# A decoder layer with two attentions: NSA's z gates computed in the phase of Strassen's products, and a third bank for NSA's logits

## The chip, the cores and the metric

The kernel runs on one core of a Trainium2 chip. PE multiplies matrices (its weight loads, PEld, run beside it), DVE and ACT work on elements, POOL and SP mostly issue DMAs here. The metric is the device time of one execution in microseconds (us); the time before is 1524.45, the median of three runs.

## The reference, cut to what matters

One layer on 512 tokens of width 2048, all in float32:

```
h   = x @ W_in                       # columns: fox q,k,v,f,z | nsa q, k,v (three branches), gates, z | merge a, b
y_a = (fox_attention(...) * silu(fox_z)) @ w_a
y_b = (nsa_attention(...) * silu(nsa_z)) @ w_b
x   = layer_norm(alpha * x + (sigmoid(merge_a) * y_a + sigmoid(merge_b) * y_b) @ w_o)
```

There are 8 heads of width 128 in each attention. NSA has two groups of four heads; a group shares its keys and values, and each head adds three branches: 31 compressed blocks, selected blocks and a window. With 512 tokens the selection and the window both see all earlier tokens. The change touches `nsa_z` (1024 columns of `W_in`, from column C_NZ), the last 256 columns of each merge gate, and the order of NSA's other projections.

## The kernel before, in words

**Numbers.** A float32 operand is kept as a high and a low part (`split`: ACT copies to the reduced format, DVE subtracts). A product is three matmuls (`mm3`): high by high, high by low, low by high. One matmul has a 128x128 stationary operand and up to 512 moving columns.

**Units.** The program is a list of units that `stream` emits in turn. A unit has a weight tile of 128x512, loaded by SP into `wr` and split into `wh`/`wl` three units ahead. `dense` (by way of `proj`) computes 128 columns of a projection for all 512 tokens, transposed (columns on partitions), as 16 k-tiles: four units of four k-tiles, 48 matmuls into one of two `d` banks, and then an evacuation function.

**Ticks.** All other work hangs on `tick()`, which `dense` calls after k-tiles 1 and 3 of each unit. A tick advances every job in `active` by one step, then the first entry of the queue `tq`, then that of `sq`. Steps are written as generators. So the order on each engine is fixed when the program is built: dense matmuls, then a tick's pieces, then dense matmuls. `drain(cond)` calls `tick` with no dense work between until a condition holds.

**A head of NSA.** `nsa_s` (in `sq`) waits for the head's q and its group's keys, and then emits eight matrix products of logits into `s` banks, one in a tick; a tick later `exp_row` (DVE adds the bias and takes the extreme, ACT the exponential), a tick later `norm_row`. `nsa_t` (in `tq`) has nine items, one in a tick: PE transposes a block of probabilities into a `pt` bank (two of them), a tick later `split_p` reads it with ACT and DVE into `pT`, two ticks later `pv` multiplies it with the values into bank `o`. At the end `gate_out` (L433) multiplies `o` with the head's gate tile `z`. In a tick a head's `pv` comes first, then `split_p`, then the next transpose.

**PSUM.** There are eight banks: `d`, `s` and `pt` two each, `o` and `m` one each. A bank is used again when the instructions that read it are done. `m` carries the transposes of V in `evac_v`.

**Gates.** silu is written as 0.5 z (1 + tanh(z/2)). Each NSA z projection comes right behind its head's q projection, and `evac_z` (L289) makes the gate from `d` with one ACT and one DVE instruction; it waits in one of five `z` tiles.

**The phase of products.** `pairs` computes 512 tokens by two column blocks of 512 (or 384), k in two halves, with Strassen's seven products in place of eight: 7 x 48 matmuls with the tokens' parts as stationary operands. DVE adds blocks of weights, POOL adds others by accumulating DMAs. Results come out by rows (tokens on partitions), pass through `zo` and are stored to DRAM by SP (`keep`). Before, it has five jobs: Fox's V into `vd`, and for each merge gate columns 0 to 1023 and 1024 to 1791 into `sig_d` after a sigmoid. The last 256 columns of each merge gate are four dense projections at NSA's end (`evac_sig`: sigmoid, four transposes into an `s` bank, ACT copy, store). Before the last of these, `o_open` (L1191) drains all jobs.

**Order.** First z of three Fox heads and raw compressed keys and values, then the phase of products, Fox, NSA, the merge (`y_chunk`), the output projection and the norm. NSA's order is q0, z0, keys and values of group 0 (`nsa_open` drains Fox first), then q and z of heads 1 to 3, keys and values of group 1, q and z of heads 4 to 7, four gate tiles. The new keys wait until the group's logits are done, the new values until its values stage is done.

Of the kernel before, what the change touches and what calls it, by code (L numbers as in the profile page):

```python
# [12 lines left out]
F32 = mybir.dt.float32  # L13
F32R = mybir.dt.float32r
AF = mybir.ActivationFunctionType
ALU = mybir.AluOpType
# [47 lines left out]
def layer(ctx, tc, x, w_in, b_f, pos_k, pos_v, wk1, wk2, wv1, wv2, w_a, w_b, w_o, ln_g, ln_b, rel, onehot, out):  # L64
# [147 lines left out]
                u["pre"] = pre  # L212
            units.append(u)

    def dense(w, ncols, col, rows, get_src, evac, pre=None, each=None):

        kts = rows // P
        st = {}

        def pe(u, k0):  # L220
            if k0 == 0:
                st["ps"] = bank("d", 2)
            hi, lo = (t.rearrange("p (k c) -> p k c", c=P) for t in u["w"])
            for k in range(4):
                if each:
                    each(k0 + k)
                mm3(st["ps"], (hi[:, k], lo[:, k]), get_src(k0 + k), k0 + k == 0, k0 + k == kts - 1)
                if k % 2 == 1:
                    tick()
            if k0 + 4 == kts:  # L230
                evac(st["ps"])

        for k0 in range(0, kts, 8):
            add_chunk(lambda r: r.rearrange("p (k c) -> p k c", c=P),
                      dram(w, k0 * P * ncols + col, [[ncols, P], [P * ncols, 8], [1, P]]),
                      lambda u, half, k0=k0: pe(u, k0 + 4 * half), pre=pre if k0 == 0 else None)
# [77 lines left out]
    def v_load(h):  # L314
# [11 lines left out]
        split(hi, lo, v)  # L326
        done.add(("v", ("f", h)))

    def evac_q(key):
        def f(p):  # L330
            take("q")
            t = pool("attn").tile([P, 2, S], F32R, name="q", tag="q", bufs=2)
            split(t[:, 0], t[:, 1], p, SC)
            qt[key] = t
            done.add(("q", key))
        return f
# [8 lines left out]
    def evac_v(key, dst):  # L345

        def f(p):
            take("vT")
            v = pool("attn").tile([P, S], F32, name="vT", tag="vT", bufs=1)
            nc.scalar.activation(v, p, AF.Copy)  # L350

            def job():
                yield
                yield
                m = bank("m", 1)
                for j in range(NT):
                    nc.tensor.transpose(m[:, j * P:(j + 1) * P], v[:, j * P:(j + 1) * P], ident)
                free["vT"] += 1
                hi, lo = dst()
                split(hi, lo, m)  # L360
                done.add(("v", key))
                yield
            active.append(job())
        return f
# [109 lines left out]
    def fox_bias(h):  # L474
# [7 lines left out]
                                    fill=NEG, base=i * P, channel_multiplier=1)  # L482
        return m

    def nsa_s(h, st):
        key, g = ("n", h), h // HPG
        yield from wait_for(("q", key), ("k", ("s", g)), ("k", ("w", g)))
        bt = pool("nsa").tile([P, S], F32, name="bt", tag="bt", bufs=2)
        nc.gpsimd.dma_start(bt, dram(skew_d, h * P * RL + P - 1, [[RL - 1, P], [1, S]]))  # L489
        yield  # L490
        st["s"], st["st"] = yield from take_p()
        st["w"], st["wt"] = yield from take_p()
        q, k = qt[key], kt_[g]
        tcm = pool("nsa").tile([P, NT, CP], F32, name="tc", tag="tc", bufs=1)

        def mm(it):
            i, br = it["i"], it["br"]
            n = (i + 1) * P
            t0 = slice(i * P, (i + 1) * P)
            b = bank("s", 2)  # L500
            it["bias"] = bt[:, (NT - 1 - i) * P:]
            if i == 0:
                def both(u):
                    return k[:, u, :2 * S].rearrange("p (b c) -> p b c", b=2)[:, :, :CP + P]
                mm3(b[:, :2 * (CP + P)].rearrange("p (b c) -> p b c", b=2), (q[:, 0, t0], q[:, 1, t0]),
                    (both(0), both(1)), True, True)
                it["b"], it["logits"] = b, b[:, CP:CP + P]
                it["other"].update(logits=b[:, 2 * CP + P:2 * (CP + P)], bias=it["bias"])
                return
            c0 = {"c": 0, "sc": 0, "s": CP, "w": CP + S}[br]  # L510
            nn = {"c": CP, "sc": CP + n, "s": n, "w": n}[br]
            mm3(b[:, :nn], (q[:, 0, t0], q[:, 1, t0]), (k[:, 0, c0:c0 + nn], k[:, 1, c0:c0 + nn]), True, True)
            it["b"] = b
            it["logits"] = b[:, CP:CP + n] if br == "sc" else b[:, :n]

        def red(it):
            if it["br"] in ("c", "sc"):
                nc.vector.tensor_tensor(tcm[:, it["i"]], it["b"][:, :CP], cb[:, h, it["i"]], op=ALU.add)
            if it["br"] != "c":
                exp_row(it)  # L520
            if "other" in it:
                exp_row(it["other"])

        def norm(it):
            if it["br"] != "c":
                norm_row(it)
            if "other" in it:
                norm_row(it["other"])

        def items(nm, n, brs):  # L530
            mn, l, r = stat("mn"), stat("l"), stat("r")
            return [dict(i=i, br=br, p=st[nm], mn=mn, l=l, r=r, gate=gates[:, i, 3 * h + n:3 * h + n + 1])
                    for i, br in brs]

        steps = items("s", 1, [(0, "sc"), (1, "sc"), (2, "sc"), (3, "c"), (3, "s")])
        other = items("w", 2, [(i, "w") for i in range(NT)])
        steps[0]["other"] = other[0]
        steps += other[1:]
        mc, lc, rc = stat("mn"), stat("l"), stat("r")
        for n, _ in enumerate(staged(steps, (mm, red, norm))):  # L540
            if n == 5:
                nc.vector.tensor_reduce(mc, tcm, axis=AX.X, op=ALU.max)
                nc.vector.tensor_tensor(tcm, tcm, mc[:, :, None].to_broadcast([P, NT, CP]), op=ALU.subtract)
                nc.scalar.activation(tcm, tcm, AF.Exp)
            if n == 7:
                nc.vector.tensor_reduce(lc, tcm, axis=AX.X, op=ALU.add)
                nc.vector.reciprocal(rc, lc)
                nc.vector.tensor_tensor(rc, rc, gates[:, :, 3 * h], op=ALU.mult)
                yield from take_later("tc")

                st["c"] = tc3 = pool("nsa").tile([P, NT, C3], F32, name="tc3", tag="tc3", bufs=1)
                nc.vector.tensor_tensor(tc3.rearrange("p i (u c) -> p i u c", u=3),
                                        tcm[:, :, None, :].to_broadcast([P, NT, 3, CP]),
                                        rc[:, :, None, None].to_broadcast([P, NT, 3, CP]), op=ALU.mult)
            if n == 7:
                done.add(("s", key))
                free["q"] += 1
            yield
        done.add(("p", key))
# [54 lines left out]
    zd = [dp.tile([P, S], F32, name=f"z_d{h}") for h in range(NZD)]  # L614
    rawd = {(kv, g): dp.tile([P, S], F32, name=f"raw_d{kv}{g}") for kv in "kv" for g in range(G)}
    vd = dp.tile([S, H * DH], F32, name="v_d")
    sigd = [dp.tile([S, D], F32, name=f"sig_d{g}") for g in range(2)]

    def tables():
# [291 lines left out]
            return t[:, 0].rearrange("p j d -> p (j d)"), t[:, 1].rearrange("p j d -> p (j d)")  # L911
        return f

    def nsa_kv(g):
        def vpre():
            drain(lambda: all(("t", ("n", h)) in done for h in range(g * HPG)))
        proj(C_KS + g * DH, evac_k(("s", g), nsa_k_dst("s", g)), pre=None if g else nsa_open)
        proj(C_KW + g * DH, evac_k(("w", g), nsa_k_dst("w", g)))
        proj(C_VS + g * DH, evac_v(("s", g), nsa_v_dst("s", g)), pre=vpre if g else None)
        proj(C_VW + g * DH, evac_v(("w", g), nsa_v_dst("w", g)))  # L920

# [196 lines left out]
    def phase_split():  # L1118
        jobs = [kept(vd, AF.Copy, C_FV, (0, S), S)]
        for g, c in enumerate((C_GA, C_GB)):  # L1120
            jobs.append(kept(sigd[g], AF.Sigmoid, c, (0, S), S))
            jobs.append(kept(sigd[g], AF.Sigmoid, c, (2 * S, 2 * S + W2), W2))
        ops = {n: t_op(n) for n in ("T1", "T2", "T3", "T4")}
        ops.update({"B11": b_op(0, 0), "B21": b_op(1, 0), "B22": b_op(1, 1)})
        pairs(jobs, ops, KT // 2, pairs_open)
# [30 lines left out]
    for kv, h in (("v", 4), ("k", 1)):  # L1156
        for n, l0 in enumerate(range(0, CMP_LEN, 2 * LB)):
            units[at[h] + 4 * n + 4:at[h] + 4 * n + 4] = cmp_units(kv, l0)
    for h in range(H):
        if h % HPG == 0 and h:  # L1160
            nsa_kv(h // HPG)
        proj(C_NQ + h * DH, evac_q(("n", h)))
        proj(C_NZ + h * DH, evac_z(("n", h)))
        if h == 0:
            nsa_kv(0)


    sig, osp, fin = {}, {}, {}

# [32 lines left out]
                    yield  # L1202
        active.append(job())

    for j in range(NG // P, KT):
        for g, c in enumerate((C_GA, C_GB)):
            proj(c + j * P, evac_sig(g, j), pre=o_open if (j, g) == (KT - 1, 1) else None)

    BANKS = [("pt", 2), ("pt", 2), ("o", 1), ("m", 1)], [("d", 2), ("d", 2), ("s", 2), ("s", 2)]

# [351 lines left out]
```

## Time and profile before

| | |
|---|---|
| median of 3 runs | 1524.45 us (1524.35 to 1525.06) |
| the profiled execution | 1525.12 us, its span 1523.4 us |
| PE busy | 1504.0 us, 99% of the span |
| DVE, ACT, POOL busy | 55%, 42%, 14% |
| granted PE clock | 0.999 |
| phase of products | 106 to 460 us |
| NSA, from the first q to the last gate tile | 767 to 1156 us |

The span is the time between the first and the last instruction; what lies around it is in the execution's time. A line of the timeline gives start, duration, engine, line of the kernel, operation, output and inputs, shape and count; in brackets stands the idle time of the engine ahead of it and who ended it. Successive matmuls overlap, so a matmul's price is the distance between two starts and not its duration. Instructions of one kind in a row are merged (x3).

### The profile page before, as it was taken

The page shows a single profiled execution, that of the slowest core. Times are in us where ns is not written, and L with a number is a line of the kernel's source. Part 1 is how long each engine was busy: PE and PEld are TensorE (multiplying, and loading weights), DVE is VectorE, ACT ScalarE, POOL GpSimd, SP SyncE. Part 2 cuts the span into 40 slices and gives each one's busy share as a digit, 9 for nine tenths or more (in the row PEclk, how much of TensorE's full clock was granted, in tenths as well). Part 3 has the DMA queues.
Part 4 walks back from the last instruction along what each step waited for, and adds up shares of the span by engine and source line. Part 5 has one row for each costly group of instructions (what it writes and reads, how often), then busy time and mean ns, then how long its engine had stood idle before and what let it go on. Part 6 is the DMA issues. An engine that isn't in the chain of part 4 may idle for free.

```text
span 1523.4 us, 19742 instructions
## 1 busy us (share of the span) xinstructions
PE 1504.0 (99%) x7161; PEld 1256.0 (82%) x7161; DVE 836.7 (55%) x1680; ACT 647.0 (42%) x1270; POOL 210.6 (14%) x351
## 2 busy tenths in 40 slices
PE   8999999999999999999999999999999999999998
PEld 6688788987998888888888888888888888888886
DVE  4566666666664654654435665366645444444455
ACT  6255656555563543533334444244444222222233
POOL 1211010111114623422000000000002010030001
PEclk9999999999999999999999999999999999999999
DMA  8678585877666443443233222322236343272236
GB/s 227 156 220 183 183 194 161 197 214 180 161 161 190 144 136 91 144 138 108 72 98 90 75 77 73 87 76 77 56 96 209 125 145 125 91 249 97 97 111 166
DMA packets 202929, 208.59 MB, mean 137 GB/s; under 512 B 12768, under 2 KB 153104, under 8 KB 202832
## 3 DMA queue, kind: packets, MB, share of 16 engines
q1 hardware_dynamic: 181936, 158.88, 34.9%
q0 software_dynamic: 20608, 47.93, 14.2%
q8 instruction: 56, 0.92, 0.2%
q10 hardware_dynamic: 288, 0.52, 0.1%
q14 instruction: 41, 0.34, 0.1%
HBM read 190.72 MB, written 20.22 MB: 138 GB/s over the span
## 4 chain that ended last, share of the span: by engine, by line
PE 92%; DVE 4%; ACT 2%; DMA 1%; issue 1%; POOL 0%; SPq 0%; ACTq 0%; DVEq 0%; POOLq 0%
PE d L105 50%; PE s L105 13%; PE pt L105 9%; PE o L105 9%; PE m L105 6%; DVE wl L97 2%; PE pt L417 2%; ACT wh L96 1%; PE m L111 1%; PE o L111 0%; PE d L1234 0%; DMA sig_d<-zo 0%; DVE c L993 0%; DVE s L992 0%; DMA vT<-v_d 0%
## 5 line engine op out<-in xcount | busy, mean ns | idle before, releaser
L105 PE MATMUL d<-big,wh 128*128 128x512 f32 x1792 | 568.7, 398 | 1.4 <-ACT wh L96 1.1
L97 DVE TENSOR_TENSOR wl<-wr,wh 128x512 fp32r<-128x512 f32 (+1 forms) x492 | 331.5, 682 | 379.1 <-ACT wh L96 368.7
L96 ACT ACTIVATE wh<-wr 128x512 fp32r<-128x512 f32 (+1 forms) x492 | 299.8, 618 | 388.5 <-PE d L105 140.0
L105 PEld LDWEIGHTS d<-big,wh 128*128 128x128 f32 x1792 | 324.1, 188 | 65.2 <-issue 2.1
L105 PE MATMUL d<-big,wl 128*128 128x512 f32 x896 | 351.5, 392 | 0.1
L105 PEld LDWEIGHTS d<-big,wl 128*128 128x128 f32 x896 | 168.5, 188 | 37.9 <-DVE wl L97 0.9
L399 ACT ACTIVATE p<-p,mn 128x128 f32<-128x128 f32 (+3 forms) x96 | 54.0, 562 | 133.5 <-DVE mn L397 133.5
L97 DVE TENSOR_TENSOR wl<-s,wh 128x512 fp32r<-128x512 f32 (+1 forms) x120 | 75.2, 637 | 54.1 <-ACT wh L96 53.9
L96 ACT ACTIVATE wh<-s 128x512 fp32r<-128x512 f32 (+1 forms) x120 | 69.0, 587 | 58.3 <-DVE wl L97 32.8
L105 PE MATMUL s<-wh,T 128*128 128x512 f32 (+1 forms) x320 | 93.2, 367 | 0.0
L105 PE MATMUL o<-wh,big 128*128 128x512 f32 (+1 forms) x224 | 84.3, 376 | 2.6 <-ACT wh L96 2.6
L105 PE MATMUL m<-wh,big 128*128 128x512 f32 (+1 forms) x224 | 83.7, 374 | 0.0
L105 PE MATMUL d<-wh,big 128*128 128x512 f32 (+1 forms) x240 | 74.4, 376 | 0.0
L97 DVE TENSOR_TENSOR pT<-pt,pT 128x512 fp32r<-128x512 f32 (+1 forms) x96 | 46.6, 488 | 44.3 <-ACT pT L96 43.9
L105 PEld LDWEIGHTS s<-wh,T 128*128 128x128 f32 x320 | 59.2, 188 | 7.5
L805 POOL TENSOR_SCALAR af<-raw,posT 128x31 f32<-128x31 f32 x128 | 65.2, 531 | 0.1
L96 ACT ACTIVATE pT<-pt 128x512 fp32r<-128x512 f32 (+1 forms) x96 | 41.2, 433 | 46.8 <-PE pt L417 46.0
L105 PE MATMUL s<-wl,T 128*128 128x512 f32 (+1 forms) x160 | 58.7, 367 | 0.0
L105 PEld LDWEIGHTS o<-wh,big 128*128 128x128 f32 x224 | 42.0, 188 | 10.6 <-ACT wh L96 4.5
L105 PEld LDWEIGHTS d<-wh,big 128*128 128x128 f32 x240 | 44.7, 188 | 7.2 <-ACT wh L96 0.4
L967 POOL DMA_DIRECT2D r<-in_w_in_dram x20 | 24.0, 1198 | 187.5 <-DVE wl L97 77.4
L489 POOL DMA_DIRECT2D bt<-skew_d x8 | 4.3, 540 | 324.9 <-DVE mn L397 257.5
(314 smaller groups left out, 2398.9 us busy)
## 6 DMA issues: line engine op xcount, KB each, us to landing
wr<-in_w_in_dram SPq DMA_DIRECT2D x147, 512.0 KB, 3.7
wr<-in_w_o_dram SPq DMA_DIRECT2D x32, 512.0 KB, 3.6
wr<-in_w_in_dram SPq DMA_DIRECT2D x24, 384.0 KB, 3.8
wr<-in_w_a_dram SPq DMA_DIRECT2D x16, 512.0 KB, 3.6
om<-sig_d POOLq DMA_DIRECT2D x32, 256.0 KB, 4.9
wr<-in_w_b_dram SPq DMA_DIRECT2D x16, 512.0 KB, 3.6
r<-in_w_in_dram SPq DMA_DIRECT2D x12, 512.0 KB, 5.3
r<-in_w_in_dram POOLq DMA_DIRECT2D x12, 512.0 KB, 10.4
```

The costliest lines, as they stand in the source:

```text
L96: nc.scalar.activation(hi, src, AF.Copy)
L97: nc.vector.tensor_tensor(lo, src, hi.bitcast(F32), op=ALU.subtract)
L105: nc.tensor.matmul(o, u, v, start=first and n == 0, stop=last and n == 2, **kw)
L111: nc.tensor.matmul(*u, start=first and u is whole, stop=last and u is whole)
L399: nc.scalar.activation(row, row, AF.Exp, bias=it["mn"][:, i:i + 1], scale=-1.0, accum_out=it["l"][:, i:i + 1])
L417: nc.tensor.transpose(b[:, (i - j) * P:(i - j + 1) * P], pt[:, OFF[i] + j * P:OFF[i] + (j + 1) * P], ident)
L489: nc.gpsimd.dma_start(bt, dram(skew_d, h * P * RL + P - 1, [[RL - 1, P], [1, S]]))
L805: nc.gpsimd.tensor_scalar(af[:, l, g], src, posT[:, po0 + ll:po0 + ll + 1], None, op0=ALU.add)
L967: nc.gpsimd.dma_start(two(n, k), rows(jobs[j], quad[0] * kh + k - 1, quad[1]), accum_op=ALU.add)
```

## The change

The eight z projections leave NSA. A sixth job of `pairs` computes nsa_z by rows and stores it, without an activation, to a new DRAM tensor `nz_d`. For each head a new job `nz_load` takes a `z` tile, loads the head's 128 columns (rows on partitions, 512 bytes each), waits four ticks, transposes four 128x128 blocks into a `pt` bank, and makes the gate as before (tanh on ACT, product on DVE). It is put into `active` ahead of the head's q projection.

NSA's projections have a new order: q0, one gate tile, keys and values of group 0, q1 to q4 with group 1's keys behind q4, q5, group 1's values, q6, q7, three gate tiles. The gate tiles and the last two q projections tick after k-tiles 1, 2 and 3. The logits take three banks in turn (`m`, `s`, `s`), and `evac_v` transposes into `pt` instead of `m`.

```diff
-    def dense(w, ncols, col, rows, get_src, evac, pre=None, each=None):
+    def dense(w, ncols, col, rows, get_src, evac, pre=None, each=None, steps=(1, 3)):
...
-                if k % 2 == 1:
+                if k in steps:
                     tick()
...
+    def rows_of(dt, ncols, col):
+        return dram(dt[:], col, [[ncols, P], [P * ncols, NT], [1, DH]])
+
+    def nz_load(h):
+        yield from take_later("z")
+        t = z_tile()
+        nc.gpsimd.dma_start(t.rearrange("p (j d) -> p j d", d=DH), rows_of(nzd, H * DH, h * DH))
+        for _ in range(4):
+            yield
+        m = bank("pt", 2)
+        for j in range(NT):
+            nc.tensor.transpose(m[:, j * P:(j + 1) * P], t[:, j * P:(j + 1) * P], ident)
+        nc.scalar.activation(t, m, AF.Tanh, scale=0.5)
+        nc.vector.scalar_tensor_tensor(t, t, 1.0, m, op0=ALU.add, op1=ALU.mult)
+        zt["n", h] = t
+        done.add(("z", ("n", h)))
+        yield
...
     def evac_v(key, dst):
...
-                m = bank("m", 1)
+                m = bank("pt", 2)
...
+    logits = [0]
+
+    def s_bank():
+        logits[0] += 1
+        return bank(*(("m", 1), ("s", 2), ("s", 2))[logits[0] % 3])
...
     def nsa_s(h, st):
...
-            b = bank("s", 2)
+            b = s_bank()
...
+    nzd = dp.tile([S, H * DH], F32, name="nz_d")
...
-    def nsa_kv(g):
+    def nsa_keys(g):
+        proj(C_KS + g * DH, evac_k(("s", g), nsa_k_dst("s", g)), pre=None if g else nsa_open)
+        proj(C_KW + g * DH, evac_k(("w", g), nsa_k_dst("w", g)))
+
+    def nsa_values(g):
...
+        jobs.append(kept(nzd, AF.Copy, C_NZ, (0, S), S))
...
-    for h in range(H):
-        if h % HPG == 0 and h:
-            nsa_kv(h // HPG)
-        proj(C_NQ + h * DH, evac_q(("n", h)))
-        proj(C_NZ + h * DH, evac_z(("n", h)))
-        if h == 0:
-            nsa_kv(0)
...
-    for j in range(NG // P, KT):
-        for g, c in enumerate((C_GA, C_GB)):
-            proj(c + j * P, evac_sig(g, j), pre=o_open if (j, g) == (KT - 1, 1) else None)
+    rest = [(j, g) for j in range(NG // P, KT) for g in range(2)]
+
+    def gate_tile(pre=None):
+        j, g = rest.pop()
+        proj((C_GA, C_GB)[g] + j * P, evac_sig(g, j), pre=pre, steps=(1, 2, 3))
+
+    for h in range(H):
+        proj(C_NQ + h * DH, evac_q(("n", h)), pre=lambda h=h: active.append(nz_load(h)),
+             steps=(1, 3) if h < H - 2 else (1, 2, 3))
+        if h == 0:
+            gate_tile()
+        if h % HPG == 0:
+            nsa_keys(h // HPG)
+        if h in (0, HPG + 1):
+            nsa_values(h // HPG)
+    while rest:
+        gate_tile(pre=o_open if len(rest) == 1 else None)
```

More of the change, by code (lines that the diff above doesn't have):

```diff
@@ L912, in nsa_v_dst @@
         return f
-    def nsa_kv(g):
+    def nsa_keys(g):
+        proj(C_KS + g * DH, evac_k(("s", g), nsa_k_dst("s", g)), pre=None if g else nsa_open)
+        proj(C_KW + g * DH, evac_k(("w", g), nsa_k_dst("w", g)))
+    def nsa_values(g):
         def vpre():
             drain(lambda: all(("t", ("n", h)) in done for h in range(g * HPG)))
-        proj(C_KS + g * DH, evac_k(("s", g), nsa_k_dst("s", g)), pre=None if g else nsa_open)
-        proj(C_KW + g * DH, evac_k(("w", g), nsa_k_dst("w", g)))
         proj(C_VS + g * DH, evac_v(("s", g), nsa_v_dst("s", g)), pre=vpre if g else None)
```

## The prediction

> **What bounds the kernel now.** I read the page first, then the waits of PE, then stretches of the timeline. The page's lines are PE's busy time, PE and its granted clock in 40 slices, and the chain that ended last.
>
> ```profile
> PE 1504.0 (99%) x7161; PEld 1256.0 (82%) x7161; DVE 836.7 (55%) x1680; ACT 647.0 (42%) x1270; POOL 210.6 (14%) x351
> PE   8999999999999999999999999999999999999998
> PEclk9999999999999999999999999999999999999999
> PE 92%; DVE 4%; ACT 2%; DMA 1%; issue 1%; POOL 0%; SPq 0%; ACTq 0%; DVEq 0%; POOLq 0%
> ```
>
> PE is busy for all but 19 us, at full clock, and is 92% of the chain. So the time changes by the matmul time that goes or comes, plus every wait that PE takes in its own order. Who PE waited for:
>
> ```profile
> PE s L1465 <- DMA xa<-in_x_dram: 4.5, 1, 4.5
> PE m L718 <- DVE facc L712: 1.3, 1, 1.3
> PE pt L417 <- DVE pT L97: 0.8, 2, 0.4
> PE s L1182 <- ACT z L1175: 0.7, 1, 0.7
> ```
>
> These are totals: PE waited only 0.8 us for a transpose bank (`pt`) in all 16 heads. NSA's stage has no slack to give back, and any new wait there is paid in full.
>
> **The matmul work.** The phase of products runs PE without holes; a 512-wide job ran twice in a row (vd, then the first of sig_d). The jobs begin where the bank changes to `pt`:
>
> ```profile
> 106.33 0.39 PE L105 MATMUL pt<-wh,T 128*128 128x512 f32 x1
> 184.12 0.39 PE L105 MATMUL pt<-wh,T 128*128 128x512 f32 x1
> 261.90 0.33 PE L105 MATMUL pt<-wh,T 128*128 128x384 f32 x1
> ```
> ```profile
> 106.33:184.12 77.79, 77.02 (x338) 62.92 (x336) 51.44 (x73) 43.56 (x72) 8.48 (x8) 1.00 0.74 187
> 184.12:261.90 77.78, 77.02 (x337) 62.92 (x336) 51.16 (x73) 44.42 (x74) 9.54 (x8) 1.00 0.71 178
> 1037.00:1070.00 33.00, 33.00 (x172) 27.95 (x171) 21.23 (x63) 14.83 (x37) 0.54 (x1) 1.00 0.28 72
> ```
>
> The columns are length, then busy time of PE, PEld, DVE, ACT and POOL. The new sixth job has the same shape (1024 columns as two blocks of 512): seven products of 48 matmuls. It costs **+77.8**, and its sums (DVE), POOL's accumulating loads, SP's reads and its eight writes to nz_d lie inside, as in these two.
>
> Eight NSA z projections of 48 matmuls go. One projection with little beside it is the last gate tile, from 1145.14 to 1156.12:
>
> ```profile
> 1143.65 0.39 PE L105 MATMUL d<-big,wl 128*128 128x512 f32 x1
> 1144.07 0.60 ACT L1175 ACTIVATE z<-d 128x512 f32<-128x512 f32 x1 [2.31 <-PE d L105]
> 1144.72 0.66 PE L1182 MATMUL s<-ident,z 128*128 128x128 f32 x4 [0.69 <-ACT z L1175]
> 1145.14 0.71 PE L105 MATMUL d<-big,wh 128*128 128x512 f32 x2
> 1145.48 0.60 ACT L1183 ACTIVATE z<-s 128x512 f32<-128x512 f32 x1 [0.81 <-PE s L1182]
> 1156.12 0.39 PE L105 MATMUL pt<-wh,osp 128*128 128x512 f32 x1
> ```
>
> That is 10.98 us (0.23 a matmul, 1.37 for the six between two ticks), so **-87.8**. Each gate is now transposed, four transposes of 128x128. Their price, from the transposes of a gate tile between other work:
>
> ```profile
> 1121.82 0.60 PE L1182 MATMUL s<-ident,z 128*128 128x128 f32 x4
> 1122.18 0.60 PE L105 MATMUL o<-pT,nvs 128*128 128x256 f32 x3
> 1122.52 0.60 ACT L1183 ACTIVATE z<-s 128x512 f32<-128x512 f32 x1 [2.45 <-PE s L1182]
> ...
> 1122.86 0.71 PE L105 MATMUL d<-big,wh 128*128 128x512 f32 x2
> 1123.01 0.59 ACT L96 ACTIVATE pT<-pt 128x512 fp32r<-128x512 f32 x1
> ```
>
> 0.36 to the next start, and the pair of dense matmuls behind transposes is shown 0.09 longer (0.71 here, 0.62 in the row of 1060.23 further down): 0.45, times eight **+3.6**. Work alone: 77.8 - 87.8 + 3.6 = **-6.4 us**.
>
> The eight loads of a gate (POOL) are issued ahead of their use by four ticks and more, since POOL stands idle in NSA's stage (0.54 us busy in the 33 us above): nothing. Nor does it count as work that eight tanh and products move from a projection's end to behind the transposes; their place in the order does, and is the next point.
>
> **Where PE now waits for a bank.** Ticks are counted through the generators. A head's values stage (`nsa_t`) takes 13 ticks: nine transposes into `pt` on ticks 1 to 9, each split one tick later, products on ticks 4 to 12. A gate is transposed on the fifth tick of its head's q projection, and this job runs ahead of `nsa_t` in the tick. Both share two `pt` banks. With KS0's first tick as 1: gates 1 to 7 fall on 37, 45, 53, 61, 86, 112 and 124; values of heads 0, 1, 3, 4, 5 transpose on 35 to 43, 53 to 61, 79 to 87, 110 to 118 and 123 to 131. So five gates (1, 4, 5, 6, 7) fall one tick behind a transpose whose bank is not yet split. Order on PE: gate's four transposes into the one free bank, perhaps a product, then the head's next transpose. That one needs a bank that is freed at the earliest by the gate's own tanh (ACT) and product (DVE), which stand ahead of the head's split on both engines. Gate 3 comes with its head's first transpose, and the dense matmuls of a tick (1.37 us) cover it; gates 0 and 2 meet none.
>
> The price of one meeting: 0.70 from the first transpose to ACT's start (1121.82 to 1122.52), 0.63 from tanh to the product and 0.69 for it (rows below), 0.05 to PE's restart (1144.67 to 1144.72): 2.07, less PE's own 0.45 and the product between.
>
> ```profile
> 1069.04 0.60 ACT L294 ACTIVATE z<-d 128x512 f32<-128x512 f32 x1
> 1069.67 0.69 DVE L295 SCALAR_TENSOR_TENSOR z<-z,d 128x512 f32<-128x512 f32 x1 [1.24 <-ACT z L294]
> ```
>
> Gates 1, 6, 7 meet no product: 1.6 each. Gate 4 has three 512-wide matmuls between (0.69): 0.9. Gate 5 has three 128-wide ones (0.28, from 1059.14 to 1059.42 further down): 1.35. Together **+7.1**. Ends: 0, if the banks free up unlike this count; 12, if each next transpose waits for the head's split too (0.69 more) and ACT is 0.3 late. Behind a waiting transpose stand the logits and the next dense matmuls, all on PE. The old z evacuation read `d`, which has two banks and never held PE.
>
> **The drains.** By the same count, ticks without dense work grow from 1 to 4 where NSA opens, 1 to 2 before VS1, 0 to 1 at KS1, 4 to 6 before the last gate tile. At NSA's opening a gate tile now ends just before: PE waits for the sigmoid as in the rows above, 1143.65 to 1144.72 instead of 0.23: **+0.85** (0.7 by that row's wait; 2.1 with a table load in front). The sigmoid's table comes twice more into ACT; ahead of it ACT stood idle for 2.31, and a load takes 1.28:
>
> ```profile
> 1114.74 1.28 ACT L1175 ACT_TABLE_LOAD   x1
> ```
>
> so nothing. [...]
>
> Before the last gate tile the wait of 0.85 was there already; now head 7's last three transposes, splits and products fill the same drain. By ACT's and DVE's order PE waits about 1.1: **+0.3** (0 to 2). The other two drains issue work whose splits are a tick old: 0.
>
> **Shorter ticks.** The last two q projections and the gate tiles tick three times per four k instead of two. While logits and values of two heads overlap, one tick hangs on a loop through ACT and DVE. In the kernel before:
>
> ```profile
> 1059.14 0.45 PE L105 MATMUL o<-pT,nvs 128*128 128x128 f32 x3
> 1059.42 0.40 PE L417 MATMUL pt<-ident,p 128*128 128x128 f32 x2
> 1059.58 0.81 PE L105 MATMUL s<-nk,q 128*128 128x416 f32 x3
> 1060.23 0.62 PE L105 MATMUL d<-big,wh 128*128 128x512 f32 x2
> ...
> 1062.34 0.49 PE L105 MATMUL s<-nk,q 128*128 128x32 f32 x3
> ...
> 1062.78 0.55 DVE L397 CUSTOM_DVE_ANT_0 p<-s,bt 128x384 f32<-128x384 f32 x1
> ...
> 1064.66 0.63 PE L105 MATMUL s<-nk,q 128*128 128x512 f32 x2
> ...
> 1065.77 0.68 DVE L397 CUSTOM_DVE_ANT_0 p<-s,bt 128x512 f32<-128x512 f32 x1
> ```
>
> DVE takes the logits of 1059.58 at 1062.78, 3.2 late, while PE's ticks are 2.5 apart (1059.58, 1062.34, 1064.66). In a short tick PE has 0.9 of dense work instead of 1.4, so some 2.0. Over the 11 overlapping short ticks (heads 6 and 7) DVE falls behind by up to 1.2 a tick; three logits banks instead of two give PE 6 us of lead, two `pt` banks 4. I take **+1.0** (0 to 4): half a microsecond for each overlap. Otherwise the third logits bank is worth nothing, since PE waited for no logits bank before; values at `pt` meet nothing (their head waits for them).
>
> **Fox's start.** ACT's split of the first v waits for POOL's load, which stands behind loads that wait for the last store of the products' phase:
>
> ```profile
> 473.75 0.63 ACT L96 ACTIVATE v<-vT 128x512 fp32r<-128x512 f32 x1 [9.88 <-DMA vT<-v_d]
> 474.96 0.73 PE L105 MATMUL d<-big,wh 128*128 128x512 f32 x2 [0.65 <-ACT wh L96]
> ```
>
> That store is now 512 wide instead of 384: **+0.3** (0 to 1).
>
> **Sum.** -6.4 + 7.1 + 0.85 + 0.3 + 1.0 + 0.3 = +3.15. The profiled execution took 1525.12 (span 1523.4 and 1.7 around it), so 1528.3; the median of the runs shown lies 0.67 lower, so **1527.6**.
>
> **Rivals.** *Faster: the banks are free in time.* If the meetings cost 0 to 2 us, the sum is -5 to -2: about 1520.5. For it: PE waited 0.8 us for `pt` before, and DVE is busy only 64% of an NSA stretch (21.23 of 33). Against: the order in a tick is fixed, and the rows of 1122.52 and 1123.01 show the split of a head's `pT` standing behind a gate's copy on ACT. *Slower: the loop of ACT and DVE bounds the short ticks.* Place: from NQ7 to the second gate tile. Each of 11 overlapping ticks at 3.2 instead of 2.0, less 4 us of lead once: +9, with the rest 1536. It decides as soon as the lag passes two ticks, when a transpose finds its `pt` bank unsplit. For it the 3.2 above; against it, the lag there fell to 1.1 two rows later. *The clock falls.* A wait that drops the granted clock would make each 512-wide matmul slower than its 0.23; the page shows full clock through waits of 4.5 and 1.3. [...] *The job is no cheaper than the projections* is excluded by two jobs at 77.8.
>
> **Chances.** Forecast 0.53, own range 1524 to 1532; banks free 0.27; loop bound 0.17; clock 0.03. Runs of this kernel tell 0.2% (3 us) from no change: slower is above 1527.5, faster below 1521.4. The forecast lies on that line, half of it slower (0.25), half the same (0.27). Of the faster rival 0.23 is faster, 0.04 the same. So faster 0.24, same 0.31, slower 0.45. The range takes in the faster rival and the forecast's upper end: 1519 to 1533.
>
> **What would show it.** The sixth job: 77.8 between two changes to `pt`. Line 105 on `d`: 384 fewer matmuls from 2688. The waits of PE: a row of the new transposes' and `pt` L417's wait for DVE's gate product, about 5 times 1 to 1.6. One more wait for a sigmoid of 0.7. Wrong would be: no wait at L417 on the gate's product (then 1520 to 1522), or waits at L417 on DVE's split in the last two heads above 5 us (then 1536).

## The result, and the profile after

| | before | after |
|---|---|---|
| median | 1524.58 us (4 runs beside the change) | 1539.78 us (4 runs, 1538.77 to 1541.24) |
| ratio | | 1.0102, 95% interval 1.009 to 1.0115 |
| profiled execution, its span | 1525.12, 1523.4 | 1541.24, 1539.2 |

The change makes the kernel 1.0% slower. The prediction had the direction with a chance of 0.45, but the time lies 6.8 us above its range. The page after, with the lines that answer to the four shown first before:

```profile
PE 1504.6 (98%) x7145; PEld 1253.2 (81%) x7145; DVE 866.4 (56%) x1720; ACT 670.6 (44%) x1312; POOL 225.6 (15%) x367
PE   8999999999999999999999999999899999999998
PEclk9999999999999999999999999999999999999999
PE 90%; DVE 5%; ACT 3%; issue 1%; DMA 0%; SPq 0%; ACTq 0%; DVEq 0%
```

PE's busy time grew by 0.6 us although 16 matmuls fewer are counted, and the span grew by 15.8. DVE and ACT went from 6% to 8% of the chain. Who PE waited for, between NSA's start and the end of the gate tiles (total, times, longest, in us):

```profile
PE pt L437 <- DVE z L344: 8.6, 6, 2.8
PE pt L437 <- DVE pT L97: 5.9, 6, 1.7
PE s L1205 <- ACT z L1198: 0.7, 1, 0.7
PE pt L437 <- DVE pT L610: 0.3, 1, 0.3
PE pt L342 <- DVE pT L610: 0.2, 1, 0.2
```

In the same stretch the kernel before had one row, its sigmoid of 0.7. The first row is the predicted one: the head's next transpose (L437) waits for the DVE product of the gate (L344), six times. The second row was predicted only as a rival: transposes that wait for the head's own split (L97). Its 5.9 us lie between 1107 and 1138 us, in the ticks of the last heads, and the prediction had named more than 5 us there as a sign that it was wrong.

The arithmetic of the matmuls came out. Fox's first projection starts 78.28 us later, the sixth job of 77.8 and half a microsecond from the kernel's start:

```profile
460.40:538.68 78.28, 77.50 (x339) 62.95 (x337) 51.93 (x73) 43.98 (x74) 10.32 (x10) 1.00 0.67 163
```

The merge, which follows NSA, starts at 1171.83 us instead of 1156.12, so 15.7 us later; its first matmul:

```profile
1171.83 0.39 PE L105 MATMUL pt<-wh,osp 128*128 128x512 f32 x1
```

So 62.6 us come back between these two points. Fox gives 1.3 of them, since a wait at its start is gone. NSA and its gate tiles (from 752.94 us before, where the first q projection starts, and from 829.95 after) give back 61.3 us of the 87.8 that their dense matmuls had taken. The other 26.5 went into the transposes (3.6), into waits and, as the next stretch shows, into a slower clock. This is the dearest meeting, gate 6, in the timeline:

```profile
1068.30 0.66 PE L342 MATMUL pt<-ident,z 128*128 128x128 f32 x4 [0.23 <-DVE pT L610]
1068.97 0.69 DVE L417 CUSTOM_DVE_ANT_0 p<-m,bt 128x512 f32<-128x512 f32 x1
1069.70 0.72 ACT L419 ACTIVATE p<-p,mn 128x512 f32<-128x512 f32 x1 [2.96 <-DVE mn L417]
1070.42 0.58 ACT L343 ACTIVATE z<-pt 128x512 f32<-128x512 f32 x1
1071.03 0.69 DVE L344 SCALAR_TENSOR_TENSOR z<-z,pt 128x512 f32<-128x512 f32 x1 [1.36 <-ACT z L343]
1071.77 0.90 PE L437 MATMUL pt<-ident,p 128*128 128x128 f32 x3 [2.82 <-DVE z L344]
1072.32 1.20 PE L105 MATMUL d<-big,wh 128*128 128x512 f32 x2
1073.32 0.63 PE L105 MATMUL d<-big,wl 128*128 128x512 f32 x1
1078.11 0.71 PE L105 MATMUL d<-big,wh 128*128 128x512 f32 x2
```

The gate's tanh (1070.42) stands on ACT behind the exponential of the next head's last logits row (1069.70), and that one behind its row on DVE (1068.97). PE waits 2.82 us. After it the pair of dense matmuls takes 1.20 instead of 0.71, and a single one 0.63 instead of 0.39; at 1078.11 they are back. The granted clock (the column behind the five busy times) says the same, here and once more behind two waits in the first of the three last gate tiles (1.12 us up to 1134.50 and 1.72 up to 1137.74):

```profile
1070.80:1077.60 6.80, 5.83 (x17) 4.66 (x18) 3.58 (x7) 2.19 (x5) 0.00 (x0) 0.50 0.36 88
1139.10:1142.50 3.40, 3.40 (x11) 2.51 (x10) 1.31 (x3) 1.22 (x4) 0.00 (x0) 0.50 0.22 58
```

The growth of the span in the prediction's own terms, each loss read as the distance between two matmul starts less what it is when nothing waits:

| term | predicted | measured |
|---|---|---|
| work alone | -6.4 | -6.4 (the job measured; the projections and transposes as priced) |
| meetings of gates | +7.1 | +10.2 |
| sigmoid where NSA opens | +0.85 | +0.85 |
| short ticks | +1.0 | +7.4 |
| drain before the last gate tile | +0.3 | -0.4 |
| Fox's start | +0.3 | -1.3 |
| clock | 0 | +4.6 |
| the kernel's start, before the phase of products | not in the sum | +0.5 |
| sum | +3.15 | +15.45 (the span grew by 15.8) |

Such a table says where the time was lost, not why. Two theories share it. By the first, each wait has its own local cause (a shared bank, a short tick), and taking the cause away returns that wait. By the second, the dense z projections had been the cover of the work on ACT and DVE in NSA; without them that work shows somewhere, and taking one meeting away moves the wait to another place. A third question is the clock. The experiments go at these.

### The profile page after: what moved, and what is told of

It is laid out like the page before. It is cut to its first block, busy times and chain, and to the rows that moved or that the text cites. A ratio compares the mean times of both kernels' runs of the same rounds, so it can differ in the third digit from the quotient of the medians.

```text
span 1539.2 us, 19884 instructions
## 1 busy us (share of the span) xinstructions
PE 1504.6 (98%) x7145; PEld 1253.2 (81%) x7145; DVE 866.4 (56%) x1720; ACT 670.6 (44%) x1312; POOL 225.6 (15%) x367
## 4 chain that ended last, share of the span: by engine, by line
PE 90%; DVE 5%; ACT 3%; issue 1%; DMA 0%; SPq 0%; ACTq 0%; DVEq 0%
PE d L105 46%; PE s L105 13%; PE pt L105 10%; PE o L105 9%; PE m L105 7%; DVE wl L97 3%; PE pt L437 2%; ACT wh L96 2%; PE m L111 1%; PE o L111 0%; PE d L1271 0%; DVE c L1023 0%; ACT p L419 0%; DVE s L1022 0%; DVE pT L97 0%
## 5 line engine op out<-in xcount | busy, mean ns | idle before, releaser
L97 DVE TENSOR_TENSOR wl<-wr,wh 128x512 fp32r<-128x512 f32 (+1 forms) x484 | 325.4, 681 | 350.2 <-ACT wh L96 338.7
L105 PE MATMUL d<-big,wh 128*128 128x512 f32 x1536 | 490.1, 400 | 0.8 <-ACT wh L96 0.4
L105 PEld LDWEIGHTS d<-big,wh 128*128 128x128 f32 x1536 | 278.5, 189 | 54.6 <-issue 2.3
L105 PE MATMUL d<-big,wl 128*128 128x512 f32 x768 | 302.4, 394 | 0.0
L105 PEld LDWEIGHTS d<-big,wl 128*128 128x128 f32 x768 | 145.2, 189 | 32.4 <-DVE wl L97 0.6
L97 DVE TENSOR_TENSOR wl<-s,wh 128x512 fp32r<-128x512 f32 (+1 forms) x144 | 91.6, 646 | 66.7 <-ACT wh L96 66.5
L96 ACT ACTIVATE wh<-s 128x512 fp32r<-128x512 f32 (+1 forms) x144 | 83.8, 594 | 72.0 <-DVE wl L97 43.7
L105 PE MATMUL s<-wh,T 128*128 128x512 f32 (+1 forms) x384 | 113.2, 371 | 0.0
L105 PE MATMUL o<-wh,big 128*128 128x512 f32 (+1 forms) x256 | 96.8, 378 | 3.1 <-ACT wh L96 3.1
L105 PE MATMUL m<-wh,big 128*128 128x512 f32 (+1 forms) x256 | 96.2, 376 | 0.0
L97 DVE TENSOR_TENSOR pT<-pt,pT 128x512 fp32r<-128x512 f32 (+1 forms) x96 | 46.5, 487 | 47.4 <-ACT pT L96 47.2
L437 PE MATMUL pt<-ident,p 128*128 128x128 f32 x240 | 44.3, 281 | 16.6 <-DVE z L344 8.6
```

Source lines behind the costliest of these rows:

```text
L96: nc.scalar.activation(hi, src, AF.Copy)
L97: nc.vector.tensor_tensor(lo, src, hi.bitcast(F32), op=ALU.subtract)
L105: nc.tensor.matmul(o, u, v, start=first and n == 0, stop=last and n == 2, **kw)
L437: nc.tensor.transpose(b[:, (i - j) * P:(i - j + 1) * P], pt[:, OFF[i] + j * P:OFF[i] + (j + 1) * P], ident)
```

## The experiments

**Gates away from `pt`, in `m`.** The gates get the bank that the logits' third had.

```diff
 def nz_load(h):
-        m = bank("pt", 2)
+        m = bank("m", 1)
 def nsa_s(h, st):
-            b = s_bank()
+            b = bank("s", 2)
```

> The changed kernel with the gates' transposes in bank m and NSA's logits on the two s banks alone. Theory A (the meetings: a head's transpose waits for the gate's product in pt): the waits of pt on the gate's product (8.6 us by the changed kernel's waits, 10.2 us of lost time in its matmul starts) go, and with the longest of them the half-clock stretch at 1071 (6.8 us long, 2.9 us of PE time): 1539.8 - 10.2 - 2.9 = 1526.7. Theory B (the loop through ACT and DVE sets the pace anyway): the waits come back at pt on DVE's splits or at the logits, and the time stays above 1536.

Measured: 1534.58 us, ratio 1.0073 (1.0056 to 1.009), 5.2 below the change, far from the 1526.7 that goes with local causes. PE's waits in NSA, without the sigmoid's 0.7:

```profile
PE pt L437 <- DVE pT L97: 3.9, 5, 1.7
PE s L105 <- DVE mn L417: 3.1, 6, 0.9
PE pt L437 <- DVE r L424: 2.7, 1, 2.7
PE pt L437 <- DVE pT L609: 0.8, 1, 0.8
```

No transpose waits for a gate's product any more: the meetings are gone, as they should be. But new rows stand there, logits that wait for a bank (3.1) and, at the place of gate 6, a wait of nearly the same length behind ACT and DVE (2.7). The edit also takes the third logits bank away; the next run looks at that alone.

**Two logits banks.** The change with `s_bank` undone and nothing else.

```diff
 def nsa_s(h, st):
-            b = s_bank()
+            b = bank("s", 2)
```

> The changed kernel with NSA's logits on two s banks again, gates still transposed in pt. Theory A (PE waits for no logits bank, the third one is worth nothing): 1539.8, within 1.5. Rival (the third bank is what keeps the short ticks going): waits of s for DVE's logits rows appear in the last two heads, +2 to +5, 1542 to 1545.

Measured: 1540.46 us, ratio 1.0105 (1.009 to 1.012), within a microsecond of the change. The third bank is worth nothing in the changed kernel, as the prediction had it, although it does remove waits. Three rows of PE's waits in NSA:

```profile
PE pt L437 <- DVE z L344: 8.2, 6, 2.8
PE pt L437 <- DVE pT L97: 3.8, 4, 1.7
PE s L105 <- DVE mn L417: 1.6, 5, 0.7
```

With two banks 1.6 us are lost at `s`, and 2.1 fewer at `pt` behind the splits. The waits changed place.

**Ticks as before.** The change with two ticks a unit everywhere.

```diff
-        proj((C_GA, C_GB)[g] + j * P, evac_sig(g, j), pre=pre, steps=(1, 2, 3))
+        proj((C_GA, C_GB)[g] + j * P, evac_sig(g, j), pre=pre, steps=(1, 3))
...
-             steps=(1, 3) if h < H - 2 else (1, 2, 3))
+             steps=(1, 3))
```

> The changed kernel with two ticks per four k-tiles everywhere. By the count of ticks the drain before the last gate tile grows from 6 to 22. Theory A (short ticks are needed, their own waits are small): 4 us of waits in the last heads go, but 16 more ticks without dense work cost about 1.5 us each: 1539.8 - 4 + 24 = about 1560. Rival (the short ticks are the main loss): below 1536.

Measured: 1537.50 us (two runs, 1536.44 and 1538.56), ratio 1.0086 (1.0066 to 1.0106). Both expectations missed. From the projection of head 7's q to the last drain the change loses 9.1 us, 7.4 in the short ticks and 1.65 at gate 7; here the same stretch loses 3.5. But the last drain, now 22 ticks long, loses 6.8 us by the starts of its matmuls, where the change loses 0.5; one wait makes up more than half of that:

```profile
PE pt L437 <- DVE pT L97: 6.3, 6, 3.8
```

So the short ticks don't pay here, and most of what they cost comes back in the longer drain. The profiled execution ran at a mean clock of 0.998, that of the change at 0.995, so the 2.3 us between the medians may be the clock's; that is not shown.

**A wait by itself.** The kernel before, where one gate tile passes four times through an ACT copy onto itself; its four transposes wait for that.

```diff
 def evac_sig(g, j):
             nc.scalar.activation(t, p, AF.Sigmoid)
+            if (j, g) == (KT - 1, 0):
+                for _ in range(4):
+                    nc.scalar.activation(t, t, AF.Copy)
```

> The kernel before with four extra ACT copies (0.57 us each, 2.3 us in all) between the sigmoid of the third gate tile and its transposes, so that PE's one wait of 0.7 us there becomes 3.0 us; nothing else is late. Theory C (a wait of some 3 us also drops the granted clock to half): 2.3 plus half of 3.4 to 6.8 us, 4.0 to 5.7 above before, 1528.6 to 1530.3, with a mean clock below 0.999. Rival (a wait costs only itself): +2.3, 1526.9, clock 0.999.

Measured: 1528.73 us (7 runs), ratio 1.0028 (1.0017 to 1.0039). The wait grew by 2.6 us (the row below against 0.7), the time by 4.2 to 4.4. The rest is the clock, in the stretch that follows the wait:

```profile
PE s L1185 <- ACT z L1178: 3.3, 1, 3.3
1148.50:1152.00 3.50, 3.50 (x10) 2.72 (x9) 1.90 (x3) 2.15 (x4) 0.62 (x2) 0.52 0.33 98
```

Behind one wait of 3.3 us in a kernel that is otherwise undisturbed stand 3.4 us at half clock, so 1.7 us of matmuls. That is the clock rival, shown by itself.

**A shorter wait.** The same with two copies.

> The kernel before with two extra ACT copies (1.15 us) at the third gate tile's transposes, so that PE's wait there is 2.0 instead of 0.85 us of lost time. In the changed kernel the clock stayed at full behind waits of 1.6 us and fell behind 3.0; with four copies (3.5 us lost) it fell for 3.4 us. If 2.0 is too short to drop it: +1.2, 1525.7, clock 0.999. If not: +2.9, 1527.4.

Measured: 1525.55 us (10 runs, 1523.9 to 1527.87), ratio 1.0008 (0.9998 to 1.0018). The runs spread over 4 us. In the profiled one the wait was 2.0 us and the clock did fall:

```profile
PE s L1185 <- ACT z L1178: 2.0, 1, 2.0
1145.30:1148.70 3.40, 3.40 (x10) 2.86 (x11) 1.07 (x2) 2.15 (x4) 0.00 (x0) 0.50 0.23 68
```

The median is 1.1 us later, which the longer wait alone (1.3) explains; with a drop it would be 3.0. Both fit together if the clock falls in some executions only. One execution was profiled, and the ten executions' mean clocks (0.998 or 0.999, as in the kernel before) don't tell them apart, so this is likely and not shown.

**Gates in a `d` bank.** Here the gates leave `pt` and the logits keep three banks: the shared bank alone is taken away.

```diff
 def nz_load(h):
-        m = bank("pt", 2)
+        m = bank("d", 2)
```

> The changed kernel with the gates' transposes in bank d (which a projection uses only every second time) and the three logits banks kept. Theory A (meetings): no transpose of a head waits for a gate's product, and no logits wait as in the version with the gates in m and two logits banks (1534.6, 5.7 us of lost time at the logits): 1529 to 1531. Theory B (ACT and DVE in their order hold the splits back whatever bank the gates use): the logits' waits turn into waits of pt on DVE's splits, 1533 to 1535.

Measured: 1533.45 us, ratio 1.006 (1.0045 to 1.0075), in the range of the second theory. That is 6.3 below the change; the meetings had shown 10.2, and the profiled execution ran at a mean clock of 0.996 instead of 0.995. PE's waits in NSA, without the sigmoid's 0.7:

```profile
PE pt L437 <- DVE pT L97: 6.3, 8, 1.7
PE pt L437 <- DVE r L424: 2.7, 1, 2.7
PE pt L437 <- DVE pT L610: 1.1, 2, 0.8
```

The waits behind the head's splits (6.3) are mostly those of the short ticks: by the starts of the matmuls they lose the same 7.4 us as in the change. At gate 6's place a wait of 2.69 us stays:

```profile
1066.53 0.69 DVE L344 SCALAR_TENSOR_TENSOR z<-z,d 128x512 f32<-128x512 f32 x1 [1.36 <-ACT z L343]
1067.13 0.68 DVE L97 TENSOR_TENSOR pT<-pt,pT 128x512 fp32r<-128x512 f32 x1
1067.96 0.66 PE L437 MATMUL pt<-ident,p 128*128 128x128 f32 x2 [2.69 <-DVE r L424]
```

The gate's bank is out of this chain, but not its work: the head's split on DVE (1067.13) still stands behind the gate's product (1066.53), and that behind the tanh (1065.92) and the same late exponential (1065.20) on ACT. And in this kernel the clock fell behind it, while behind the same 2.69 us in the kernel with the gates in `m` it did not; the section on the hardware comes back to that.

**Gates in `d`, ticks as before.** Both edits together.

> The same with two ticks per four k-tiles everywhere. The even ticks alone took 1537.5 although the drain before the last gate tile has 22 ticks instead of 6, so a tick of that drain costs some 0.4 us of waits and not 1.5. Theory A: the meetings with gates 1, 3, 4, 5 and 7 go (6.4 us of lost time there), the long wait at gate 6 stays in part: 1530 to 1531. Theory B: 1534 or more.

Measured: 1531.42 us, ratio 1.0048 (1.0033 to 1.0063). Here local causes came nearer, 0.4 us above their range and 2.6 below the other theory's. This is the best version found of the change, and it is still slower than the kernel before. The largest piece of what is left is the drain before the last gate tile, and the clock after it:

```profile
1136.57 0.66 PE L437 MATMUL pt<-ident,p 128*128 128x128 f32 x4 [3.83 <-DVE pT L97]
1137.30:1140.70 3.40, 3.25 (x16) 3.04 (x15) 1.25 (x3) 1.70 (x4) 0.00 (x0) 0.50 0.26 80
```

**The job alone.** The kernel before, with its order, ticks and banks; only the eight z projections are replaced by the sixth job, the loads and the transposes (in `d`).

```diff
+        jobs.append(kept(nzd, AF.Copy, C_NZ, (0, S), S))
...
-        proj(C_NQ + h * DH, evac_q(("n", h)))
-        proj(C_NZ + h * DH, evac_z(("n", h)))
+        proj(C_NQ + h * DH, evac_q(("n", h)), pre=lambda h=h: active.append(nz_load(h)))
```

> The kernel before with the z gates alone moved (sixth job, loads, transposes in bank d); the order of NSA, the gate tiles, ticks, two logits banks and V's transposes in m as before. If the loss comes from the change's new order and short ticks, this is near the matmul work alone, 1524.5 - 6.4 + 2 = 1520. If the dense z projections were the cover of the background work (theory B), their loss shows in any order: by the count of ticks the drains grow from 1, 0, 1, 4 to 9, 9, 10, 16, 38 ticks more at about 0.4 us each, and the time is 1530 to 1536.

Measured: 1538.49 us, ratio 1.0089 (1.0074 to 1.0104), above both ranges. No gate shares a bank with a head's transposes here, no tick is short, no tile was moved, and still:

```profile
PE pt L437 <- DVE pT L97: 4.3, 7, 1.1
PE s L105 <- DVE mn L417: 3.8, 7, 1.0
PE pt L437 <- DVE p L428: 1.9, 1, 1.9
PE pt L437 <- DVE pT L603: 1.8, 2, 1.1
PE o L105 <- DVE pT L97: 0.6, 2, 0.3
```

The work alone gives 1524.4 - 6.4 = 1518.0; the kernel takes 20.5 more. 12.4 of it are these rows, all behind splits, rows and norms of the heads themselves; some 5 are two stretches at a clock of 0.50 (847.0 to 850.4 and 973.3 to 980.1 us), and the rest is in gaps too short for a row. Counted through the generators, its four drains have 9, 9, 10 and 16 ticks where the kernel before has 1, 0, 1 and 4: the heads' steps no longer fit beside the dense work. The timeline bears this out. Four times, from 7.2 to 16.8 us long, no matmul of a projection runs (843 to 851, 967 to 984, 998 to 1005 and 1146 to 1158 us); 9.4 of the 12.4 us and both stretches at half clock lie in these. The kernel before has no such stretch above 4 us. The change's new order and third bank bring this to 1531.42; with the short ticks as well it is 1533.45, and with the gates in `pt` too 1539.78.

**The cover put back.** The last kernel, with the eight dense projections again where they were; their results are thrown away, and the gates still come from the sixth job.

```diff
         proj(C_NQ + h * DH, evac_q(("n", h)), pre=lambda h=h: active.append(nz_load(h)))
+        proj(C_NZ + h * DH, lambda p: None)
```

> The kernel of e7, with the eight dense projections of NSA's z put back where the kernel before has them. Their results are thrown away: the gates still come from the sixth job of the products. So every load, transposition, tanh and product of the gates is still there, and the only thing that differs from e7 is matmuls that fill the TensorE. Theory B (the dense projections were the cover of the work on ScalarE and VectorE): the waits of NSA fall back towards those of the kernel before (about 1 us between 760 us and the end of NSA as against 12 us in e7), and the time is that of the kernel before plus the job and the transpositions, 1524.4 + 77.8 + 3.6 = 1605.8, within 3 us. Theory A (the gates' own work holds up the TensorE where it stands, whatever matmuls are beside it): the waits of e7 stay, about 12 us and a drop or more of the clock, and the time is e7's plus the 87.8 us of the projections, about 1626; anything above 1616 speaks for A.

Measured: 1605.90 us (two runs, 1605.34 and 1606.47), against 1605.8 expected by the theory of the cover. All that PE waits for in NSA and the gate tiles:

```profile
PE s L1204 <- ACT z L1197: 0.7, 1, 0.7
PE pt L437 <- DVE pT L97: 0.2, 1, 0.2
```

The loads, transposes, tanh and products of all gates run there, and they cost nothing beyond the priced transposes. So the gates' own work doesn't hold PE up while dense matmuls run beside it. Putting in 87.8 us of matmuls cost 1605.90 - 1538.49 = 67.4 us: the other **20.4 us** they hid (good to about 2 us by the spread of the runs). The projections bring two things back at once, matmuls to run over the heads' steps and eight ticks each to run them in; the two were not tested apart.

## Why the prediction was right or wrong

**The matmul work** (right as arithmetic). The job took 77.8, and the transposes of the eight gates fit the 3.6 of the prediction in the last experiment (1605.90 is 1524.49 + 77.8 + 3.6 to 0.01, closer than the runs' spread warrants).

**The step that failed: "work alone -6.4" as a gain that arrives.** The prediction looked for new waits only where the change touched something: a shared bank, a drain, a short tick. It took matmuls that leave NSA as pure gain. It had the row that speaks against this, PE waiting 0.8 us for `pt` in 16 heads, and read it as "no slack to give back". But the slack was the dense work itself. The pair of the last two kernels shows it, in the order of the kernel before: matmuls worth 87.8 us, their results thrown away, make 67.4 us of time. In the terms of the sum the error stands in three places: the short ticks (+1.0, measured 7.4), the clock (0, measured 4.6) and the meetings (+7.1, measured 10.2). A warning stood in a row that the prediction showed, DVE taking logits 3.2 us late. It used that row for the eleven short ticks alone, and put them at +1.0 all the same.

**Meetings of gates in `pt`.** Right for gates 1, 4, 5 and 7: 1.62, 0.88, 1.34 and 1.65 us against 1.6, 0.9, 1.35 and 1.6. This is the head's next transpose behind gate 1:

```profile
915.66 0.60 PE L342 MATMUL pt<-ident,z 128*128 128x128 f32 x4
916.30 0.60 ACT L343 ACTIVATE z<-pt 128x512 f32<-128x512 f32 x1 [1.87 <-PE pt L342]
916.93 0.69 DVE L344 SCALAR_TENSOR_TENSOR z<-z,pt 128x512 f32<-128x512 f32 x1 [1.78 <-ACT z L343]
917.67 0.55 PE L437 MATMUL pt<-ident,p 128*128 128x128 f32 x3 [1.41 <-DVE z L344]
```

Wrong for two. Gate 6 lost 3.4 instead of 1.6: the price had tanh start 0.70 after the first transpose, and in the rows of 1068.30 to 1070.42 it is 2.12, because the next head's last logits row stood ahead of it. By the code that row stands behind a step that waits for a tile (`tc`), which the first transpose of the head whose values are running has to free; that was read and not tested. Gate 3, put at 0, lost 1.28: on DVE its product stood behind a norm and a split of weights, and the "dense matmuls of a tick" that were to cover it were too few. But the sum of these prices is not what the shared bank is worth: with the gates in `d` 6.3 of the change's 15.2 return, at a mean clock of 0.996 instead of 0.995, and 2.69 us of gate 6's wait stay behind the work on ACT and DVE.

**Short ticks** (the term furthest off). +1.0 was put, 7.4 measured: two waits that cost 1.53 and 1.34 by the starts of the matmuls, three below 0.5, and two of 1.28 and 1.93 at the end of the first of the three last gate tiles. These are the idle times of the two ends:

```profile
1109.08 0.44 PE L437 MATMUL pt<-ident,p 128*128 128x128 f32 x2 [1.32 <-DVE pT L97]
1112.09 0.33 PE L437 MATMUL pt<-ident,p 128*128 128x128 f32 x1 [1.17 <-DVE pT L97]
1134.50 0.55 PE L437 MATMUL pt<-ident,p 128*128 128x128 f32 x3 [1.12 <-DVE pT L97]
```

The mechanism is the rival's (the loop of ACT and DVE), at four fifths of its price of 9, and the term lay well above its own bound of 4. The sign that the prediction had set for it came too: waits of L437 on DVE's split in the last heads of 5.9 us, above 5. But with even ticks the same stretch still loses 3.5 of 9.1 us, so the ticks' length isn't all of the cause, and the longer drain takes most of the rest: the time falls by 2.3 with the gates in `pt` and by 2.0 with the gates in `d`.

**The last drain.** +0.3 (0 to 2) was put. From the last dense matmul (1156.35) to the next (1160.89) two distances between starts are 0.20 and 0.27 too long, where the kernel before lost 0.85, so -0.4.

**The clock.** A chance of 0.03 was put on it, with the argument that the page shows full clock through waits of 4.5 and 1.3 us. The 4.5 us stand at the kernel's start, and the timeline of the kernel before shows what follows them:

```profile
6.39 1.63 PE L105 MATMUL d<-big,wh 128*128 128x512 f32 x2
7.82 0.63 PE L105 MATMUL d<-big,wl 128*128 128x512 f32 x1
```

0.63 for a matmul is what the rows behind gate 6 show at a clock of 0.50, though the clock's column says 1.00 in this stretch (the trace has no record of the clock before 11.14 us). The argument fell on two rows that were there to be read. In the experiment with four copies 3.4 us at half clock cost 1.7 us; in the change there were two drops, of 6.83 and 3.41 us, and they cost 4.6 us.

**Right, too:** the sigmoid where NSA opens (0.85), the third logits bank worth nothing, the table loads at nothing, the loads of the gates by POOL at nothing. Wrong in sign, but small: Fox's start was put 0.3 later; the wait of 0.65 there vanished instead, worth 1.3 by the starts of the matmuls (the second projection took 12.18 us before and takes 10.91).

**What stays open.** The 20.4 us belong to the order of the kernel before. How they divide in the changed order between loops in the ticks, drains and clock can't be read from sums of waits, since these change place. Whether other dense work (of the merge, say) could be put into NSA as cover was not tried.

## What to carry to other kernels

When one engine is busy throughout and others run chains beside it, matmuls that go can be worth less than their time: first ask what was running under them, and count how many steps of the chains are left over when they are gone. Here 87.8 us of matmuls hid 20.4 us. A wait that is removed at one place, in a stage whose chain is too long, can come back in part at the next; price the chain and not the place.

## What the runs showed of the hardware that was not expected

The length of PE's longest wait did not settle whether the granted clock fell. These stretches are shown at half clock, each in the one profiled execution of its kernel:

| kernel | half clock, us | granted clock | PE's waits before its start or across it, us |
|---|---|---|---|
| the change | 1070.82 to 1077.64 | 0.50 | 2.82 up to 1071.77 |
| the change | 1139.08 to 1142.50 | 0.50 | 1.12 up to 1134.50, 1.72 up to 1137.74 |
| four copies | 1148.5 to 1152.0 | 0.52 | 3.33 up to 1147.55 |
| two copies | 1145.3 to 1148.7 | 0.50 | 2.01 up to 1145.26 |
| gates in `d` | 1067.3 to 1070.7 | 0.50 | 2.69 up to 1067.96 |
| gates in `d`, ticks as before | 1137.3 to 1140.7 | 0.50 | 3.83 up to 1136.57 |
| the job alone | 973.3 to 980.1 | 0.50 | 0.77 up to 970.24, 0.78 up to 972.78 |

In the change the two drops last 6.83 and 3.41 us, and their starts lie 68.27 us apart, 20.0 times 3.41. In the job alone the stretches at half clock start 126.3 us apart (847.0 and 973.3), 37.0 times 3.41. These are two distances in two executions.

In the change PE was idle for 2.09 of the 3.42 us before 1070.82 and for 1.72 of the 3.41 us before 1139.08. In the job alone no wait in the 3.3 us before 973.3 reached 0.8 us. And behind the 1.41 us up to 917.67 in the change the clock stayed at 1.00.

The same wait of 2.69 us came out both ways. With the gates in `d` the granted clock went from 1.00 to 0.50:

```profile
1063.90:1067.30 3.40, 1.37 (x8) 0.85 (x7) 1.99 (x6) 2.10 (x6) 0.55 (x1) 1.00 0.18 39
1067.30:1070.70 3.40, 2.74 (x8) 2.28 (x9) 2.53 (x6) 0.96 (x3) 0.00 (x0) 0.50 0.16 46
```

With the gates in `m` the matmuls behind it kept their 0.71 for a pair and 0.39 for a single one:

```profile
1070.14 0.41 PE L437 MATMUL pt<-ident,p 128*128 128x128 f32 x2 [2.69 <-DVE r L424]
1070.30 0.71 PE L105 MATMUL d<-big,wh 128*128 128x512 f32 x2
1070.85 0.39 PE L105 MATMUL d<-big,wl 128*128 128x512 f32 x1
```

What decides between the two was not shown, nor was why two of the drops lasted 6.8 us and the others 3.4. Executions of one kernel differ, too: the four of the kernel with the gates in `m` ran at mean clocks of 0.995 to 0.998.
